# The second down projection of a decoder trunk as seven block products per group of 1024 hidden rows

## The chip, the cores and the metric

The kernel runs on one core of one Trainium2 chip. The core has five engines that run side by side, each with its own queue of instructions: PE (TensorE, matmuls), DVE (VectorE), ACT (ScalarE), POOL (GpSimd) and SP (SyncE, which here only issues DMAs). The metric is the device time of one execution in microseconds; a kernel is run several times and the median is given. Besides, one execution is profiled, and all durations of single instructions come from it.

## What is computed

The reference is a decoder trunk of two layers over 512 positions and 1024 channels. Each layer runs a token mixer (a gated DeltaNet in the first, a Conformer convolution module in the second), a cross-attention into a fixed memory and a squared-ReLU MLP; a last RMSNorm ends it. The change touches only the MLP of the second layer and the last norm behind it:

```python
def rms_norm(x, g):
    xf = x.astype(jnp.float32)
    y = xf * lax.rsqrt(jnp.mean(xf * xf, axis=-1, keepdims=True) + RMS_EPS)
    return (y * g.astype(jnp.float32)).astype(x.dtype)

def sq_relu_mlp(h, w_up, w_down):              # w_up 1024 x 4096, w_down 4096 x 1024
    return jnp.square(jax.nn.relu(h @ w_up)) @ w_down

# in reference(), for every layer
        h = h + sq_relu_mlp(rms_norm(h, mlp_norm[layer]), mlp_w_up[layer], mlp_w_down[layer])
# after the last one
    return rms_norm(h, final_norm)
```

## The kernel before

Activations lie with channels on the 128 partitions and the 512 positions ("tokens") along the free axis, so the residual is eight tiles of 128x512. Every float32 operand of a large product is split into a high part (rounded to fp32r by a copy on ACT) and a low part (the difference, on DVE); `mm3` (L236) then makes three matmuls of each product: high by high, low by high, high by low. `proj` (L246) runs `mm3` over the eight contraction tiles: 24 matmuls of 128x512 for one output tile. `split` (L275) makes the two parts of an activation tile.

Weights come as units of 128x1024 float32 (512 KB). `wload` (L197) issues the DMA of a unit from the SP queue into a tile named `raw`, of which there are `NRAW` = 3; `wsplit` (L205) makes the high part `wh` on ACT and the low part `wl` on DVE, of which there are `NW` = 3 each; `wnext` (L226) hands the next unit out and runs loads and splits ahead of it: the split of a unit stands two units ahead of its use, and needs the `wh` and `wl` tiles of the unit three before it. `plan`, `plan_mlp` (L165) and the lists around them set the order of the units. The engines' own order is made by the tile framework's scheduler, which keeps each engine first in, first out.

`mlp` (L1008) is called for both layers. The 4096 hidden channels are four groups of 1024. `MLP_ORDER` (L1562) is up 0, up 1, down 0, up 2, down 1, up 3, down 2, down 3, so that a group's down projection never follows directly on its own up projection. Each up step makes eight output tiles; `up_ev` takes one out of PSUM with a multiply by the norm's factor and a maximum with zero (DVE), squares it (ACT) and splits it (ACT, DVE). Each down step of eight output tiles adds one group's part to the residual with one DVE add per tile.

The last down step of the second layer is `finish` (L1497). There the products have the tokens on the output's partitions: the hidden tile's 128-token slices are the stationary operand and the weights, repacked in blocks of 512 output channels, are the moving one. Its order is `LAST` (L1488), eight tiles of (128 tokens) x (512 channels): four transposes with the identity bring the residual into the same PSUM bank, 24 matmuls add the product, then the final norm: a sum of squares (ACT), the root (ACT), its reciprocal and the multiply by it and by `gt` (DVE), and two DMAs to the output per token block. `load` (L1491) brings the weights of this step, outside of `wnext`.

## Time and profile before

| | us |
|---|---|
| median of 3 runs | 1502.38 |
| lowest and highest run | 1501.81, 1502.51 |
| span of the profiled execution, first to last instruction | 1500.9 |
| second MLP with the final norm, by the trace | 1142.3 to 1500.9 |

| engine | busy us | instructions |
|---|---|---|
| DVE | 894.9 | 1318 |
| ACT | 685.1 | 1202 |
| POOL | 212.2 | 223 |

The busy time of PE is made of matmuls whose ends are modelled, and matmuls overlap: one 128x512 matmul is shown as 0.39 us long, while the next starts 0.23 us after it. So PE's pace is read from the distance of starts, not from the mean duration. A group's line names the line of the source, the engine, the operation, the tiles (out<-in), the shape and the count, then busy us and the mean ns of one, and behind the second bar the engine's idle time before these instructions and what ended it. A line can be that of a helper: `tt` is L69, `stt` is L72.

### The profile page before, as it was taken

How to read it: one execution, taken by the hardware profiler on the slowest of the kernel's cores; microseconds unless marked ns; L12 is line 12 of the kernel's file. 1: busy time of each engine (PE TensorE's matmuls, PEld its weight loads, DVE VectorE, ACT ScalarE, POOL GpSimd, SP SyncE). 2: the span in 40 equal slices, each digit the busy share in tenths (PEclk: the TensorE clock that was granted, in tenths of full speed). 3: DMA queues.
4: the chain of work that ended last, by engine and by line, in shares of the span. 5: the costliest groups of instructions: out<-in, count | busy, mean ns of one | idle time of the engine just before them, and what ended most of it. 6: DMA issues, size and time to landing. Idle time of an engine off the chain costs nothing.

```text
span 1500.9 us, 19205 instructions
## 1 busy us (share of the span) xinstructions
PE 1492.3 (99%) x7458; PEld 1258.5 (84%) x7458; DVE 894.9 (60%) x1318; ACT 685.1 (46%) x1202; POOL 212.2 (14%) x223
## 2 busy tenths in 40 slices
PE   9999999999999999999999999999999999999998
PEld 7888889888888888888888889988888888888886
DVE  6889888867555543444445799976555543434441
ACT  7856765555444432322324464564444431423332
POOL 1411311102111000000002496211111000000000
PEclk9999999999999999999999999999999999999999
DMA  6231223522212332222233524532122222232321
GB/s 240 83 120 57 68 88 113 174 94 88 79 48 96 99 98 98 98 99 97 92 123 130 190 88 140 170 123 98 57 71 90 93 98 98 98 98 99 98 99 56
DMA packets 50059, 155.65 MB, mean 104 GB/s; under 512 B 6320, under 2 KB 8624, under 8 KB 49968
## 3 DMA queue, kind: packets, MB, share of 16 engines
q1 hardware_dynamic: 49536, 153.90, 30.7%
q8 instruction: 58, 0.95, 0.3%
q10 hardware_dynamic: 432, 0.52, 0.1%
q14 instruction: 33, 0.27, 0.1%
HBM read 151.52 MB, written 2.10 MB: 102 GB/s over the span
## 4 chain that ended last, share of the span: by engine, by line
PE 96%; ACT 2%; DVE 1%; issue 0%; DMA 0%; POOL 0%; SPq 0%; DVEq 0%
PE up L238 8%; PE up L240 8%; PE up L239 8%; PE dn L240 7%; PE dn L238 7%; PE dn L239 7%; PE pw L240 3%; PE pw L239 3%; PE pw L238 3%; PE h L238 3%; PE h L239 2%; PE h L240 2%; PE xo L239 2%; PE q L238 2%; PE xo L240 2%; PE q L240 2%
## 5 line engine op out<-in xcount | busy, mean ns | idle before, releaser
L214 ACT CAST wh<-raw 128x1024 fp32r<-128x1024 f32 x247 | 259.2, 1051 | 598.1 <-PE dn L239 190.4
L69 DVE TENSOR_TENSOR wl<-raw,wh 128x1024 fp32r<-128x1024 f32 (+1 forms) x238 | 290.9, 1224 | 82.9 <-ACT wh L214 76.7
L240 PE MATMUL up<-xh,wl 128*128 128x512 f32 x512 | 199.2, 389 | 0.0
L239 PE MATMUL up<-xl,wh 128*128 128x512 f32 x512 | 199.2, 389 | 0.0
L238 PE MATMUL up<-xh,wh 128*128 128x512 f32 x512 | 199.2, 389 | 0.0
L240 PE MATMUL dn<-uh,wl 128*128 128x512 f32 x448 | 174.3, 389 | 0.0
L238 PE MATMUL dn<-uh,wh 128*128 128x512 f32 x448 | 174.3, 389 | 0.0
L239 PE MATMUL dn<-ul,wh 128*128 128x512 f32 x448 | 174.3, 389 | 0.0
L69 DVE TENSOR_TENSOR h<-dn,h 128x512 f32<-128x512 f32 x56 | 41.8, 747 | 165.3 <-PE dn L240 165.3
L72 DVE SCALAR_TENSOR_TENSOR rl<-up,rb 128x512 f32<-128x512 f32 x64 | 44.2, 691 | 153.8 <-PE up L240 153.7
L69 POOL TENSOR_TENSOR sq<-sq,sq 128x512 f32<-128x512 f32 x30 | 49.3, 1644 | 485.9 <-ACT sq L331 475.6
L240 PEld LDWEIGHTS up<-xh,wl 128*128 128x128 f32 x512 | 96.1, 188 | 20.0
L239 PEld LDWEIGHTS up<-xl,wh 128*128 128x128 f32 x512 | 96.1, 188 | 20.0
L238 PEld LDWEIGHTS up<-xh,wh 128*128 128x128 f32 x512 | 96.1, 188 | 19.9
L239 PEld LDWEIGHTS dn<-ul,wh 128*128 128x128 f32 x448 | 84.1, 188 | 17.6
L240 PEld LDWEIGHTS dn<-uh,wl 128*128 128x128 f32 x448 | 84.1, 188 | 17.4
L238 PEld LDWEIGHTS dn<-uh,wh 128*128 128x128 f32 x448 | 84.1, 188 | 17.4
L1148 DVE SCALAR_TENSOR_TENSOR ca<-x,prm,ca 128x512 f32<-128x512 f32 x112 | 82.3, 752 | 3.6 <-ACT ca L1145 1.3
L238 PE MATMUL h<-xh,wh 128*128 128x512 f32 x184 | 73.7, 400 | 0.0
L240 PE MATMUL h<-xh,wl 128*128 128x512 f32 x184 | 71.9, 391 | 0.0
L239 PE MATMUL h<-xl,wh 128*128 128x512 f32 x184 | 71.7, 390 | 0.0
L72 DVE SCALAR_TENSOR_TENSOR cva<-cv,prm,cva 128x512 f32<-128x512 f32 x60 | 48.3, 830 | 11.5 <-POOL cva L69 10.3
(364 smaller groups left out, 3037.4 us busy)
## 6 DMA issues: line engine op xcount, KB each, us to landing
raw<-w_up SPq DMA_DIRECT2D x64, 512.0 KB, 3.5
raw<-w_dn SPq DMA_DIRECT2D x64, 512.0 KB, 3.4
raw<-w_pw SPq DMA_DIRECT2D x24, 512.0 KB, 3.5
raw<-w_k SPq DMA_DIRECT2D x16, 512.0 KB, 3.6
raw<-w_vv SPq DMA_DIRECT2D x16, 512.0 KB, 3.6
raw<-w_q SPq DMA_DIRECT2D x16, 512.0 KB, 3.3
raw<-w_o SPq DMA_DIRECT2D x16, 512.0 KB, 3.6
raw<-w_kq SPq DMA_DIRECT2D x15, 512.0 KB, 3.6
```

What stands on the lines that cost most here:

```text
L69: return e.tensor_tensor(out=o, in0=a, in1=b, op=op)
L72: return dve.scalar_tensor_tensor(out=o, in0=a, scalar=s, in1=b, op0=op0, op1=op1)
L214: ins = [act.copy(h, raw)]
L238: pe.matmul(ps, wh, xh, start=first, stop=False)
L239: pe.matmul(ps, wh, xl, start=False, stop=False)
L240: pe.matmul(ps, wl, xh, start=False, stop=last)
L1148: first["tap"] = dve.scalar_tensor_tensor(out=a, in0=src, scalar=w, in1=a, op0=ALU.mult, op1=ALU.add)
```

## The change

The second layer's MLP gets a function of its own, `mlp7`, in place of `mlp` with `finish`. The order becomes up 0, down 0, up 1, down 1, up 2, down 2, up 3, down 3. All four down steps now have the tokens on the output's partitions.

In a down step the 512 tokens are halved (blocks 1 and 2 of the left factor's rows), the 1024 hidden rows of the group are halved (the inner dimension; `w_up` is packed in another order so that hidden tiles alternate between the halves), and the 1024 output channels are halved. With left blocks a11, a12, a21, a22 and weight blocks b11 to b22 the four output blocks come from seven products in the form of Strassen and Winograd:

- S1 = a21 + a22, S2 = S1 - a11, S3 = a11 - a21, S4 = a12 - S2 (POOL, four operations of 128x256 for each pair of hidden tiles, in `operands`)
- T1 = b12 - b11 (DVE), T3 = b22 - b12, T2 = T3 + b11, T4 as b21 - T2 (POOL; each 128x1024, and each in two halves, in `combos7`)
- products in the order of `ORDER7`: a11 b11, S1 T1, S2 T2, S4 b22, S3 T3, a12 b21, a22 T4 (with the sign turned). Each has 24 matmuls of 128x512: two weight units of twelve. They accumulate in three pairs of PSUM banks (keys "a", "c", "b"), and `after` reads partial sums out between products and joins them with the running output `acc` (ACT copies, POOL and DVE adds).

Each of the seven right factors is split into high and low parts in two units, so a group's down step splits 14 units where it split 8. The residual is transposed tile by tile in `turn`, behind the up tiles of group 0 (eight times four transposes, as many as `finish` had). The final norm stands in `final`, which works on the SBUF tile that `done` has made with one more DVE add. The raw tiles become `RAWB` = 6 for the whole kernel; each is asked for as late in the plan as before, but a DMA can start up to three tiles earlier. T2's second half and `gt` take a raw tile too.

```diff
-    raw0 = wp.tile([P, 1024], F32, tag="raw", name="raw0", bufs=NRAW)
+    raw0 = wp.tile([P, 1024], F32, tag="raw", name="raw0", bufs=RAWB)
...
+    def plan_mlp7(layer):
+        for g in range(4):
+            for i in range(4):
+                plan(("up", layer, g * 4 + i), w_up[layer, g * 4 + i])
+            n = base7[g] = len(loads)
+            for b, h in LOADS7:
+                loads.append(w_dn[layer, g * 4 + "11 21 12 22".split().index(b)][:, h * 1024:(h + 1) * 1024])
+            at = {bh: n + i for i, bh in enumerate(LOADS7)}
+            for u in range(14):
+                order.append((("dn7", g), u))
+                need.append(max([at[bh] for bh in NEEDS7[ORDER7[u // 2][1]](u % 2)] + need[-1:]))
...
     def wsplit():
...
-        raw = ws["raw"].pop(u)
+        (kind, i, *j), hf = order[u]
+        raw = combos7(i, hf) if kind == "dn7" else ws["raw"].pop(need[u])
...
-        while ws["load"] < min(i + NRAW + 2, len(order)):
+        while ws["load"] <= need[min(i + NRAW + 1, len(order) - 1)]:
             wload()
...
+    def combos7(g, u):
+        raw, (name, h) = ws["raw"], (ORDER7[u // 2][1], u % 2)
...
+        if name == "11":
+            T7["3", h] = fs("t3")
+            tt(pool, T7["3", h], b("22"), b("12"), ALU.subtract)
+            T7["2", h] = fs("t2") if h == 0 else raw_tile("t2")
+            tt(pool, T7["2", h], T7["3", h], b("11"), ALU.add)
+            return b("11")
+        if name == "T1":
+            t = raw.pop(base + LOADS7.index(("12", h)))
+            tt(dve, t, t, raw.pop(base + LOADS7.index(("11", h))), ALU.subtract)
+            return t
...
+        if name == "21":
+            t = b("21")
+            tt(pool, T7["2", h], t, T7["2", h], ALU.subtract)
+            return raw.pop(base + LOADS7.index(("21", h)))
...
+    def mlp7(layer, norm, hres):
...
+        def turn(i):
+            n, m, c = i // 4, i // 2 % 2, i % 2
+            ps, a = psum("hT"), slot(s="acc")
             for j in range(4):
+                pe.transpose(ps[:, j * P:(j + 1) * P], hres[4 * m + j][:, n * 256 + c * P:n * 256 + c * P + P], ident)
+            act.copy(a, ps)
+            acc[n, m, c] = a
...
+        def operands(u0, u1):
+            o = {}
+            a11, a21, a12, a22 = u0[:, 0:256], u0[:, 256:512], u1[:, 0:256], u1[:, 256:512]
+            x, y = slot(s="s12"), slot(s="s34")
+            tt(pool, x[:, 0:256], a21, a22, ALU.add)
+            tt(pool, x[:, 256:512], x[:, 0:256], a11, ALU.subtract)
+            tt(pool, y[:, 256:512], a12, x[:, 256:512], ALU.subtract)
+            tt(pool, y[:, 0:256], a11, a21, ALU.subtract)
+            o["12"], o["22"] = pair(split(u1, "a"))
+            o["S1"], o["S2"] = pair(split(x, "s"))
+            o["S3"], o["S4"] = pair(split(y, "s"))
+            return o
+
+        def plain(u0):
+            t = slot(F32R, "a11")
+            act.copy(t[:, 0:256], u0[:, 0:256])
+            tt(dve, t[:, 256:512], u0[:, 0:256], t[:, 0:256].bitcast(F32), ALU.subtract)
+            return [t[:, 0:256], t[:, 256:512]]
+
+        def dn7(g, ops):
...
+                for h in range(2):
+                    w = wnext(("dn7", g), 2 * i + h)
+                    for c in range(2):
+                        ps = bank[key][c]
+                        for kk in range(2):
+                            k, s = 2 * h + kk, slice(kk * 512, kk * 512 + 512)
+                            xh, xl = [t[:, c * P:(c + 1) * P] for t in ops[k][left]]
+                            pe.matmul(ps, xh, w[0][:, s], start=opens and k == 0, stop=False, skip_group_check=True)
+                            pe.matmul(ps, xl, w[0][:, s], start=False, stop=False, skip_group_check=True)
+                            pe.matmul(ps, xh, w[1][:, s], start=False, stop=k == 3, skip_group_check=True)
+                        if h == 1:
+                            after(i + 1, c, ps)
...
+            def done(n, m, c, ps, other):
+                acc[n, m, c] = added(dve, ps, other, "acc")
+                if g == 3:
+                    final(n, m, c)
+
+            def after(i, c, ps):
+                if i == 1:
+                    t1 = slot(s="t1")
+                    act.copy(t1, ps)
+                    st["12", c] = added(pool, t1, acc[0, 1, c], "v12")
+                    st["t1", c] = t1
+                elif i == 2:
+                    t5 = slot(s="t5")
+                    act.copy(t5, ps)
+                    t = added(pool, t5, acc[1, 1, c], "v22")
+                    st["22", c] = added(pool, t, st["t1", c], "w22")
+                elif i == 3:
+                    st["12", c] = added(dve, ps, st["12", c], "u2")
+                    st["21", c] = added(pool, st["t1", c], acc[1, 0, c], "v21")
+                elif i == 4:
+                    done(0, 1, c, ps, st["12", c])
+                elif i == 5:
+                    done(1, 1, c, ps, st["22", c])
+                elif i == 6:
+                    done(0, 0, c, ps, acc[0, 0, c])
+                else:
+                    done(1, 0, c, ps, st["21", c])
...
+        def final(n, m, c):
+            x = acc[n, m, c]
...
+            act.activation(slot(s="fq"), x, AF.Square, accum_out=ss)
...
+            act.activation(sd, ss, AF.Sqrt, bias=b, scale=1.0 / 1024)
             dve.reciprocal(rc, sd)
+            act.activation(y1, y1, AF.Copy, scale=rc)
+            stt(y, x, rc, gt[0][:, gs], ALU.mult, ALU.mult)
...
+        for g in range(4):
+            ops, us = [{} for _ in range(4)], []
+            for i in range(8):
+                w = wnext(("up", layer, g * 4 + i // 2), i % 2)
+                ps = psum("up")
+                proj(w, xs, ps, inside={1: norm.stat} if (g, i) == (0, 1) else None)
...
+                if g == 0 and i > 1:
+                    turn(i - 2)
+            if g == 0:
+                turn(6)
+                turn(7)
...
+            dn7(g, ops)
...
+RAWB = 6
+LOADS7 = [(_b, _h) for _h in range(2) for _b in ("11", "12", "22")] + [("21", 0), ("21", 1)]
+ORDER7 = [("11", "11", "a", True), ("S1", "T1", "c", True), ("S2", "T2", "b", True), ("S4", "22", "c", False),
+          ("S3", "T3", "b", False), ("12", "21", "a", False), ("22", "T4", "b", False)]
...
-    nc = _bacc.Bacc("TRN2", target_bir_lowering=False, num_devices=1)
+    nc = _bacc.Bacc("TRN2", target_bir_lowering=False, num_devices=1, dynamic_dma_scratch_size=1024)
```

More of the change, by code (lines that the diff above doesn't have):

```diff
@@ L142, in tile_trunk, with put @@
     pool.memset(eps_ln, LN_EPS)
-    order, srcs = [], {}
+    order, srcs, loads, need = [], {}, [], []
+    def put(key, hf, src=None):
+        order.append((key, hf))
+        loads.append((srcs[key] if src is None else src)[:, hf * 1024:(hf + 1) * 1024])
+        need.append(len(loads) - 1)
     def plan(key, src, n=2):
@@ L192, in tile_trunk, with raw_tile @@
     plan_x(1)
-    plan_mlp(1, True)
+    plan_mlp7(1)
     ws = {"next": 0, "split": 0, "load": 1, "raw": {0: raw0}, "hl": {}}
+    def raw_tile(s="raw"):
+        return wp.tile([P, 1024], F32, tag="raw", name=nm(s), bufs=RAWB)
     def wload():
         u = ws["load"]
-        key, hf = order[u]
         ws["load"] += 1
-        raw = wp.tile([P, 1024], F32, tag="raw", name=nm("raw"), bufs=NRAW)
-        nc.sync.dma_start(out=raw, in_=srcs[key][:, hf * 1024:(hf + 1) * 1024])
+        raw = raw_tile()
+        nc.sync.dma_start(out=raw, in_=loads[u])
         ws["raw"][u] = raw
@@ L1005, in xattn, with mlp @@
         return new
-    def mlp(layer, norm, hres, nxt, mid=None, end=None, pre=None):
+    def mlp(layer, norm, hres, nxt, mid):
         xs = norm.xs
@@ L1021, in mlp @@
         for kind, g in MLP_ORDER:
-            if (kind, g) == ("dn", 3) and mid is not None:
+            if (kind, g) == ("dn", 3):
                 mid()
-            if (kind, g) == ("dn", 3) and end is not None:
-                return end(hid[3], cur)
             for i in range(8):
@@ L1533 @@
+    mlp7(1, n5, h)
 NSLOT = 69
@@ L1649, in _layout @@
     r["w_o"] = np.stack([_pack_a(np, i["xa_w_o"][j]) for j in range(2)])
[L1650 to L1651 removed]
+    halves = [8 * g + m for g in range(4) for m in (0, 4, 1, 5, 2, 6, 3, 7)]
+    r["w_up"] = np.stack([_pack_a(np, i["mlp_w_up"][j], halves if j else None) for j in range(2)])
+    r["w_dn"] = np.stack([np.concatenate([(_pack_b if j else _pack_a)(
         np, i["mlp_w_down"][j][g * 1024:(g + 1) * 1024]) for g in range(4)]) for j in range(2)])
```

117 lines of the change are left out of this document (68 added, 49 removed).

## The prediction

> **What bounds the kernel now.** I read the page first: the busy lines, the clock and the chain that ended last.
>
> ```profile
> PE 1492.3 (99%) x7458; PEld 1258.5 (84%) x7458; DVE 894.9 (60%) x1318; ACT 685.1 (46%) x1202; POOL 212.2 (14%) x223
> PEclk9999999999999999999999999999999999999999
> PE 96%; ACT 2%; DVE 1%; issue 0%; DMA 0%; POOL 0%; SPq 0%; DVEq 0%
> ```
>
> PE makes 96% of the chain at full clock, DMA and the SP queue 0%. Whether it is also dense in the second MLP, the timeline and the groups of 1131 to 1456 us say.
>
> ```profile
> 1142.33 0.39 PE L238 MATMUL up<-xh,wh 128*128 128x512 f32 x1
> ...
> 1152.35 0.39 PE L238 MATMUL up<-xh,wh 128*128 128x512 f32 x1
> ...
> 1157.79 0.39 PE L238 MATMUL up<-xh,wh 128*128 128x512 f32 x1
> ...
> 1459.67 0.48 PE L1510 MATMUL dn<-wdh,uh 128*128 128x512 f32 x1
> ...
> 1465.02 0.39 PE L1512 MATMUL dn<-wdl,uh 128*128 128x512 f32 x1
> ...
> 1465.60 0.47 PE L1510 MATMUL dn<-wdh,uh 128*128 128x512 f32 x1
> ...
> 1494.61 0.39 PE L1512 MATMUL dn<-wdl,uh 128*128 128x512 f32 x1
> ```
>
> The second and third row are 24 matmuls apart: 5.44 us, 0.2267 us each. The next three frame one tile of `finish`: 24 matmuls and four transposes in 5.93 us, so the transposes cost 0.49. The MLP's 64 tiles of 24 matmuls make 348.2 us, the norm's two matmuls 0.5, eight times 0.49 is 3.9: 352.6. From the first row to the end of the last one's slot, 1494.84, are 352.5: there is not one hole. The token-first form runs at the same pace as the other. What a matmul less saves here is 0.2267 us, as long as everything else keeps up.
>
> ```profile
> L69 DVE TENSOR_TENSOR wl<-raw,wh 128x1024 fp32r<-128x1024 f32 x56 | 68.6, 1225 | 14.8 <-ACT wh L214 14.7
> L214 ACT CAST wh<-raw 128x1024 fp32r<-128x1024 f32 x56 | 59.0, 1053 | 194.8 <-PE up L239 94.7 <-PE dn L239 87.5 <-issue 12.6
> L69 DVE TENSOR_TENSOR ul<-u,uh 128x512 fp32r<-128x512 f32 x32 | 22.1, 692 | 2.8 <-ACT uh L277 2.7
> L277 ACT CAST uh<-u 128x512 fp32r<-128x512 f32 x32 | 19.9, 622 | 1.0
> L72 DVE SCALAR_TENSOR_TENSOR rl<-up,rb 128x512 f32<-128x512 f32 x32 | 22.1, 691 | 76.9 <-PE up L240 76.8
> L69 DVE TENSOR_TENSOR h<-dn,h 128x512 f32<-128x512 f32 x24 | 16.6, 691 | 73.8 <-PE dn L240 73.8
> ```
>
> ACT waits for PE to give `wh` back before nearly every split, and DVE's `rl` and `h` wait for PE: both have room.
>
> **What goes from PE.** Before, a down step has 8 x 24 = 192 matmuls, after it 7 x 24 = 168: 4 x 24 = 96 fewer, 96 x 0.2267 = 21.8 us. The transposes move from the end to group 0 and stay 32: 0.
>
> The Trainium skill, "TensorE: Matmul & The Clock Gate", section "Wait — 56ns, not 53.3ns?", gives a warm matmul N/2.4 GHz plus about 2.5 ns, 215.8 ns at N = 512; by it the saving is 20.7 us, an estimate. The trace's 226.7 differs and decides.
>
> **What comes on DVE, ACT and POOL.** Per group DVE has 22 `wl` (27.0), two T1 halves (2.5), eight `rl` (5.5), twelve splits of 128x512 and four of 256 (9.7) and ten adds from PSUM (6.9): 51.6 us in a group of 43.5 + 38.1 = 81.6 (15 x 5.44). ACT has 22 x 1.053 and some 16 of smaller work, 39. For POOL the trace has these rows, in the whole kernel, in the window 1131 to 1456, and in a stretch where DVE is full:
>
> ```profile
> L69 POOL TENSOR_TENSOR wl<-raw,wh 128x1024 fp32r<-128x1024 f32 x13 | 31.1, 2403 | 9.3 <-ACT wh L214 9.3
> L69 POOL TENSOR_TENSOR ca<-ca,cvp 128x512 f32<-128x512 f32 x30 | 42.7, 1423 | 30.9 <-ACT cvp L1133 23.3 <-ACT cvp L1131 6.1
> L69 POOL TENSOR_TENSOR pexp<-pexp,sm 128x512 f32<-128x512 f32 x16 | 17.7, 1108 | 123.0 <-DVE sm L937 123.0
> L69 POOL TENSOR_TENSOR sq<-sq,sq 128x512 f32<-128x512 f32 x2 | 3.5, 1766 | 7.3 <-ACT sq L331 7.3
> 884.00:908.00 24.00, 24.00 (x124) 20.34 (x123) 23.47 (x34) 13.58 (x28) 21.45 (x13) 1.00 0.25 79
> L1148 DVE SCALAR_TENSOR_TENSOR ca<-x,prm,ca 128x512 f32<-128x512 f32 x27 | 19.8, 752 | 0.5
> ```
>
> A 1024-wide operation (A): 2.40 by the same shape, up to 2 x 1.77 = 3.53. A 256-wide one (B) has no row: half of a 512-wide one, 0.55 to 0.89; I take 0.7. Per group 6 A, 16 B and eight of 512: 37 us, at most 50, of 81.6. No engine becomes the bound by its sum; what counts is who waits in a queue.
>
> **A weight unit lasts half as long.** In a down step a unit now feeds 12 matmuls, 2.72 us, not 5.44. Its split may start when the unit three before is done, two units (5.44 us) before its use, and takes 1.05 + 1.23 + about 0.2 of hand-over: 2.5. Cover 2.9 us, less what stands ahead of it. In the built order those are at most two ACT copies (t1, t5; 1.2) or two DVE adds (1.4). I cost it at 0; with the cover gone, each late microsecond shows.
>
> **The step from up to down.** Before, a whole up step lay between the last `up_ev` of a group and its first use. Now the down step follows at once. Counting from the start of an up step (group 1 on), the weight half (22, 1) takes the raw tile of up unit 7, whose split begins when unit 4 is done, 27.2; it ends at 29.7, and with 3.4 us of DMA
>
> ```profile
> raw<-w_dn SPq DMA_DIRECT2D x64, 512.0 KB, 3.4
> ```
>
> it is there at 33.2. POOL's queue is then T3, three S operations of the third pair, T2, the fourth S: 33.2 + 2A + 4B. Behind that S stands ACT's copy of it (0.62), behind this on DVE its low part (0.69), the `rl` of up tile 6 (0.69) and `wl` of down unit 1 (1.23): 3.45 with hand-overs. PE needs that `wl` for the third matmul of unit 1, at 43.5 + 2.72 + 0.45 = 46.7. So nothing is late if 2A + 4B is under 10.0. With my values it is 7.6, at the upper ends 10.6: 0.6 to 0.8 late in each group, some 3 us in all. The last pair's S1 is needed 39 matmuls (8.8 us) into the down step; `rl`, square, three B, ACT and DVE end at about 6. In group 0 three of the transposes stand before the down step and give 1.5 us more. Bounds 0 to 3; I take 0.5, since the row of the same shape says 0.
>
> **The end.** These are the last instructions before:
>
> ```profile
> 1495.03 0.60 ACT L1514 ACTIVATE fq<-dn 128x512 f32<-128x512 f32 x1 [5.22 <-PE dn L1512]
> 1495.53 0.19 ACT L1514 ACTIVATION_READ_ACCUMULATOR fq<-dn 128x1 f32 x1
> 1495.75 0.29 ACT L1523 ACTIVATE sm<-sm,sm 128x1 f32<-128x1 f32 x1
> 1496.08 0.16 DVE L1524 RECIPROCAL sm<-sm 128x1 f32<-128x1 f32 x1 [5.49 <-ACT sm L1523]
> 1496.35 0.75 DVE L72 SCALAR_TENSOR_TENSOR y<-dn,sm,gt 128x512 f32<-128x512 f32 x1
> 1497.12 0.33 SPq L1528 DMA_DIRECT2D yT<-y  x1
> ```
>
> PE ends at 1495.0, the last multiply at 1497.1: 2.1 us; the rest (DMA, end) stays. Afterwards four tiles are normed last, two of product 6 and two of product 7. DVE's built order is add, reciprocal, multiply, four times over, so the next add waits for the last tile's root on ACT. One turn: add 0.69 and hand-over 0.1, then 2.07 as above: 2.86. The first add stands behind the `wl` of the last unit (13), whose `wh` tile is free at 11 x 2.72 = 29.9 from the start of the down step; 1.05 on ACT, and on DVE it follows `wl` 12 and a `y`: it ends at about 32.5. Then 32.5 + 4 x 2.86 = 43.9, against PE's end at 38.1: 5.8, or 3.7 more than before. From below, if only the last two turns chain: the first tile ends six matmuls before PE, -1.36 + 2 x 2.86 + 0.1 = 4.5, 2.4 more. From above, DVE's add of product 5 waits for POOL: T4 half 0 waits for a DMA at 16.9 (its raw tile is that of b22, free after unit 6), and T4 twice and four adds at 3.53 and 1.77 end at 31.1; `wl` 13 then ends near 34.8: 6.0 more.
>
> **Six raw tiles.** Up to the second MLP the built order of PE, DVE, ACT and POOL is unchanged, only SP issues weights earlier. With DMA at 0% of the chain: 0, from -1 to +1.
>
> **Sum**, against the profiled execution: 1500.9 - 21.8 + 0.5 + 3.7 = 1483.3. The runs lie 1502.38 - 1500.9 = 1.5 above it: 1484.8. By its bounds (saving 21.8; tail 2.4 to 6.0; step 0 to 3; loads -1 to 1) 1482.0 to 1491.6.
>
> **Rivals.** *POOL and DVE get in each other's way at the step from up to down.* If DVE instructions with two inputs and POOL could not run at once, POOL's queue after 33.2 would also wait for DVE's `wl`, T1 and two low parts, 1.23 + 1.23 + 1.38 = 3.8: 7.6 + 3.8 = 11.4, 1.4 late, and the last pair as much again: about 2 to 3 per group, 10 in all: 1495. Against it: in the 24 us above POOL is busy 21.45, and DVE 23.47, 19.8 of that in `ca` with two inputs at 752 ns, no longer than the 0.75 us of the multiply at 1496.35, when POOL is idle. Chance 0.13, with all slower POOL rows.
>
> The rule behind it is in the Trainium skill, "SBUF — State Buffer", section "Who interferes with whom": the two share a port pair that one holds for a whole instruction, the other fully blocks. The trace does not agree: 21.45 and 23.47 do not fit in 24.00 one after the other.
>
> *The split of weights becomes the bound of the down steps.* Three `wh` tiles, so a unit takes at least a third of (2.72 + split time). At 2.5 that is 1.7, hidden under 2.72. It decides from 5.44 on, and the gain is gone when a unit takes 17.6 / 56 = 0.31 more, 3.03, at a split time of 6.4. At 7 it is 3.24: 56 x 0.52 = 29.1, so 1484.8 + 29.1 = 1514. For it: 24 more splits, and DVE adds that wait for POOL stand ahead of `wl` in one queue. Against it: 4.5 us of waiting in every unit, on an engine with 51.6 of 81.6 filled. Chance 0.10.
>
> *The gain is eaten*, a unit late by 0.3 us or every step by 4: 1502, chance 0.05.
>
> **How the numbers follow.** Forecast 0.72, with its own range 1481.5 to 1491; rivals 0.13, 0.10, 0.05. The range reaches to the first rival: 1481.5 to 1496, leaving out the two last and some of the first. What this measurement can tell from no change is about 0.2%, 3 us. Faster 0.72 + 0.13 = 0.85; of the last case 0.04 is within the 3 us, 0.01 beyond, so same 0.04 and slower 0.11.
>
> **What would show it.** Right: up and down matmuls 0.227 us apart over all of the MLP, about 1142 to 1473; idle DVE and ACT still waiting for PE; four turns of add, reciprocal and multiply of 2.9 us at the end, PE ending 5.8 us before the last multiply and some 9.6 before the end of the span. Wrong: holes on PE behind ACT's or DVE's splits at unit 1 of a down step (the step), or every 2.72 us (the splits); POOL's 1024-wide operations over 3.5 us; DVE's `wl` well over 1.23; a change before 1142.

## The result, and the profile after

| | before | after |
|---|---|---|
| median of 4 runs, us | 1502.29 | 1509.57 |
| lowest to highest, us | 1501.81 to 1502.51 | 1509.19 to 1509.70 |
| span of the profiled execution, us | 1500.9 | 1508.0 |

The changed kernel takes 1.0050 times as long, with a 95% interval of 1.0036 to 1.0064: slower by half a per cent, where 1484.8 us and faster were forecast. Its page has these three lines, the busy times, the granted clock and the chain that ended last:

```profile
PE 1480.8 (98%) x7362; PEld 1243.9 (82%) x7362; DVE 1019.0 (68%) x1390; ACT 736.2 (49%) x1274; POOL 413.8 (27%) x343
...
PEclk9999999999999999999999999999999999999999
...
PE 83%; DVE 5%; POOL 4%; ACT 3%; issue 3%; DMA 1%; DVEq 0%; POOLq 0%
```

PE had 96% of the chain before. The 96 matmuls are gone (7458 to 7362), but 17% of the chain now lies outside PE, with DVE and POOL ahead of all others. The page's clock digits hide what happens: a slice of 38 us rounds a stretch of 3 us away.

Two rows of the timeline, the first and the last matmul of the MLP, give its length, 354.54 us in place of 352.28 before:

```profile
1141.67 0.39 PE L291 MATMUL up<-xh,wh 128*128 128x512 f32 x1
...
1496.21 0.39 PE L1595 MATMUL dn<-wl,ah 128*128 128x512 f32 x1
```

Without a hole it would be 352.28 - 21.77 = 330.51, so 24.0 us are lost inside the MLP. Behind the last matmul's start lie 1508.0 - 1496.21 = 11.8 us, before 1500.9 - 1494.61 = 6.3: 5.5 more. And the MLP starts 0.7 earlier. -21.8 + 24.0 + 5.5 - 0.7 = +7.0, against +7.1 between the spans.

The groups by line and shape between 1142 and 1508 us, with busy time and mean ns of one behind the first bar, show what became slow:

```profile
L69 DVE TENSOR_TENSOR wl<-raw,wh 128x1024 fp32r<-128x1024 f32 x62 | 99.7, 1619 | 9.6 <-ACT wh L234 9.4
...
L69 DVE TENSOR_TENSOR wl<-t,wh 128x1024 fp32r<-128x1024 f32 x24 | 43.2, 1820 | 5.2 <-ACT wh L234 5.2
...
L69 DVE TENSOR_TENSOR sl<-s,sh 128x512 fp32r<-128x512 f32 x32 | 33.2, 1041 | 28.9 <-ACT sh L330 27.4
...
L69 POOL TENSOR_TENSOR t<-raw,t 128x1024 f32<-128x1024 f32 x8 | 27.3, 3418 | 0.0
...
L69 POOL TENSOR_TENSOR s<-u 128x256 f32<-128x256 f32 x16 | 20.6, 1290 | 0.0
...
L69 POOL TENSOR_TENSOR t<-raw,raw 128x1024 f32<-128x1024 f32 x8 | 20.6, 2572 | 29.5 <-DMA raw<-w_dn 28.0 <-DVE sl L69 1.5
```

`wl` took 1225 ns before, now 1619 and 1820 on average; a low part of 512 columns goes from 692 to 1041. POOL's 1024-wide operations are 2572 to 3418 (taken at 2400), its 256-wide ones up to 1290 (taken at 700). DVE and POOL are slow together.

How that reaches PE is to be followed in group 2, whose up step starts at 1321.99. First the middle of that step, on DVE, POOL and ACT:

```profile
1339.36 2.69 POOL L69 TENSOR_TENSOR t<-raw,raw 128x1024 f32<-128x1024 f32 x1 [0.95 <-DVE sl L69]
...
1340.31 2.82 DVE L69 TENSOR_TENSOR wl<-raw,wh 128x1024 fp32r<-128x1024 f32 x1
...
1342.13 3.26 POOL L69 TENSOR_TENSOR t<-t,raw 128x1024 f32<-128x1024 f32 x1
...
1343.06 2.62 DVE L69 TENSOR_TENSOR a<-u,a 128x256 fp32r<-128x256 f32 x1
...
1347.44 0.63 ACT L1554 ACTIVATE u<-rl 128x512 f32<-128x512 f32 x1 [2.66 <-DVE rl L72]
```

The four operations pass in turn: T3 ends at 1342.05, `wl`, which began inside it, at 1343.13, T2, which began inside that, at 1345.39, and DVE's difference of 256 columns, which takes 0.42 elsewhere, at 1345.68. DVE has lost 1.6 and 2.2 us, `rl` of the next tile is late, and ACT has waited 2.66 us for it. The S of that pair, ACT's copies of it and the `wh` behind them all move back (the four S operations run from 1348.16 to 1351.80 and the copies from 1351.01), and the split of up unit 7, whose tile the half (22, 1) takes over, ends 32.9 us after the start of the step, not 29.7. The rest of the chain follows in the timeline, from the DMA that SP issues when that split is done:

```profile
1354.94 18.81 SPq L221 DMA_DIRECT2D raw<-w_dn  x3
...
1358.70 2.39 POOL L69 TENSOR_TENSOR t<-raw,raw 128x1024 f32<-128x1024 f32 x1 [6.90 <-DMA raw<-w_dn]
...
1361.04 0.74 POOL L69 TENSOR_TENSOR s<-u,u 128x256 f32<-128x256 f32 x1
...
1361.74 1.72 POOL L69 TENSOR_TENSOR s<-u 128x256 f32<-128x256 f32 x1
...
1363.42 1.18 POOL L69 TENSOR_TENSOR s<-s,u 128x256 f32<-128x256 f32 x1
...
1364.57 2.40 POOL L69 TENSOR_TENSOR t<-t,raw 128x1024 f32<-128x1024 f32 x1
...
1366.93 1.19 POOL L69 TENSOR_TENSOR s<-u,s 128x256 f32<-128x256 f32 x1
...
1368.15 0.62 ACT L330 CAST sh<-s 128x512 fp32r<-128x512 f32 x1 [2.89 <-POOL s L69]
...
1368.67 1.04 ACT L234 CAST wh<-raw 128x1024 fp32r<-128x1024 f32 x1
```

The DMA lands at 1358.70, 36.7 after the start and not 33.2; the four S operations take 4.83 and not 2.8. ACT waits for the fourth, and the weights of unit 1 stand behind it. PE, in the same stretch:

```profile
1368.01 0.39 PE L1595 MATMUL dn<-wl,a 128*128 128x512 f32 x1
1369.77 0.50 PE L1593 MATMUL dn<-wh,a 128*128 128x512 f32 x1 [1.37 <-ACT wh L234]
...
1371.28 0.50 PE L1595 MATMUL dn<-wl,a 128*128 128x512 f32 x1 [0.78 <-DVE wl L69]
...
1372.41 0.63 PE L1595 MATMUL dn<-wl,a 128*128 128x512 f32 x1
1372.84 0.63 PE L1593 MATMUL dn<-wh,a 128*128 128x512 f32 x1
```

Two holes of 1.53 and 0.94 us, and after them starts 0.43 apart, not 0.227. The view by windows, whose column before the last two is the granted clock, says why:

```profile
1371.60:1375.00 3.40, 3.40 (x10) 2.63 (x9) 3.19 (x5) 2.74 (x4) 2.01 (x2) 0.51 0.57 176
1375.20:1379.00 3.80, 3.80 (x18) 3.13 (x18) 2.38 (x3) 1.96 (x3) 2.35 (x2) 1.00 0.68 227
```

For 3.4 us the clock was 0.51: ten matmuls lie in them, wholly or in part, and eighteen in the 3.8 us after. At half pace 3.4 us hold 1.7 us of work, so the two holes, 2.5 us, cost up to another 1.7. The changed kernel has four such stretches in the MLP, one in each group.

Group 0 lost more than group 2. The four down steps take 46.41, 42.74, 42.40 and 44.77 us from their first matmul to the next up step (the last one to its last matmul's start). The kernel with everything on DVE, shown further down, needs 38.19, 38.08, 38.08 and 37.85. So 8.2, 4.7, 4.3 and 6.9 us were lost, 24.1 in all. In group 0, whose down step starts at 1189.32, PE stands at units 0, 1 and 3; the two longest waits:

```profile
1195.86 0.50 PE L1595 MATMUL dn<-wl,a 128*128 128x512 f32 x1 [1.83 <-DVE wl L69]
...
1203.36 0.50 PE L1593 MATMUL dn<-wh,sh 128*128 128x512 f32 x1 [2.15 <-ACT wh L234]
```

The `wl` that the first row waits for stands on DVE behind two low parts that take 3.80 us beside T2. The `wh` of the second row stands on ACT behind the copies of the last pair's S, which POOL makes from 1197.81 to 1201.71. Besides, `turn`'s copies of the transposes stand in ACT's queue behind a copy of S, and PE waits 0.98 us for one of them at unit 0.

### The profile page after: what moved, and what is told of

Read it like the earlier page. It is cut to its first block, busy times and chain, and to the rows that moved or that the text cites. A ratio compares the mean times of both kernels' runs of the same rounds, so it can differ in the third digit from the quotient of the medians.

```text
span 1508.0 us, 19404 instructions
## 1 busy us (share of the span) xinstructions
PE 1480.8 (98%) x7362; PEld 1243.9 (82%) x7362; DVE 1019.0 (68%) x1390; ACT 736.2 (49%) x1274; POOL 413.8 (27%) x343
## 4 chain that ended last, share of the span: by engine, by line
PE 83%; DVE 5%; POOL 4%; ACT 3%; issue 3%; DMA 1%; DVEq 0%; POOLq 0%
PE up L291 5%; PE up L292 5%; PE up L293 5%; PE dn L293 4%; PE dn L291 4%; PE dn L292 4%; PE pw L291 3%; PE pw L293 3%; PE pw L292 3%; POOL s L69 3%; PE dn L1595 3%; PE dn L1594 3%; PE dn L1593 3%; PE h L291 3%; PE h L292 2%
## 5 line engine op out<-in xcount | busy, mean ns | idle before, releaser
L234 ACT CAST wh<-raw 128x1024 fp32r<-128x1024 f32 x255 | 267.6, 1051 | 473.5 <-PE up L292 124.5
L69 DVE TENSOR_TENSOR wl<-raw,wh 128x1024 fp32r<-128x1024 f32 (+1 forms) x246 | 324.5, 1323 | 77.7 <-ACT wh L234 71.2
L291 PE MATMUL dn<-uh,wh 128*128 128x512 f32 x256 | 99.6, 389 | 0.0
L292 PE MATMUL dn<-ul,wh 128*128 128x512 f32 x256 | 99.6, 389 | 0.0
L293 PE MATMUL dn<-uh,wl 128*128 128x512 f32 x256 | 99.6, 389 | 0.0
L69 DVE TENSOR_TENSOR h<-dn,h 128x512 f32<-128x512 f32 x32 | 25.2, 788 | 91.5 <-PE dn L293 91.5
L292 PEld LDWEIGHTS dn<-ul,wh 128*128 128x128 f32 x256 | 48.1, 188 | 10.1
L293 PEld LDWEIGHTS dn<-uh,wl 128*128 128x128 f32 x256 | 48.1, 188 | 9.9
L291 PEld LDWEIGHTS dn<-uh,wh 128*128 128x128 f32 x256 | 48.1, 188 | 9.9
```

The source lines that it names most:

```text
L69: return e.tensor_tensor(out=o, in0=a, in1=b, op=op)
L234: ins = [act.copy(h, raw)]
L291: pe.matmul(ps, wh, xh, start=first, stop=False)
L292: pe.matmul(ps, wh, xl, start=False, stop=False)
L293: pe.matmul(ps, wl, xh, start=False, stop=last)
```

## The experiments

Below, "S" stands for all S operations, "T" for T2, T3 and T4, and "the adds" for POOL's eight of 512 columns per group. "MLP" in the table is the distance from the first up matmul to the last down matmul in each profile, as above; the ratio is to the kernel before in the same set of runs.

| kernel | MLP us | median us | ratio, 95% interval |
|---|---|---|---|
| before | 352.28 | 1502.29 | |
| after | 354.54 | 1509.57 | 1.0050 (1.0036 to 1.0064) |
| S on DVE | 334.34 | 1489.02 | 0.9906 (0.9890 to 0.9923) |
| T on DVE | 352.63 | 1506.82 | 1.0028 (1.0017 to 1.0039) |
| S and T on DVE | 332.05 | 1487.11 | 0.9897 (0.9882 to 0.9911) |
| after, other order at the end | 353.50 | 1506.60 | 1.0028 (1.0017 to 1.0038) |
| S and T on DVE, other order at the end | 331.86 | 1484.94 | 0.9880 (0.9864 to 0.9897) |
| T half 1 behind S in POOL's queue | 350.50 | 1506.87 | 1.0028 (1.0017 to 1.0040) |
| everything on DVE, other order at the end | 330.41 | 1482.62 | 0.9876 (0.9861 to 0.9891) |
| the same, S alone back on POOL | 345.92 | 1499.29 | 0.9979 (0.9969 to 0.9988) |
| the same, T alone back on POOL | 346.15 | 1498.71 | 0.9979 (0.9970 to 0.9989) |
| before with six raw tiles | 352.28 | 1502.61 | 1.0003 (0.9994 to 1.0011) |

**Work taken from POOL.** The first three move S, then T, then both:

```diff
-            tt(pool, x[:, 0:256], a21, a22, ALU.add)
+            tt(dve, x[:, 0:256], a21, a22, ALU.add)
...
-            tt(pool, T7["3", h], b("22"), b("12"), ALU.subtract)
+            tt(dve, T7["3", h], b("22"), b("12"), ALU.subtract)
```

> The changed kernel with the four S operations of each pair (sums and differences of hidden tiles) on DVE, not POOL; T2, T3, T4 and the eight 512-wide adds stay on POOL. Theory A (the loss in the MLP is the first weight units of each down step: S of the last pairs stands behind T3, which waits for a DMA, in POOL's queue; ACT's copy of S and DVE's low part stand behind that in theirs, and each hole of over 1.5 us on PE is followed by some 3.4 us of matmuls at half pace): with the S operations out of POOL's queue, at least two thirds of the 24.0 us lost in the MLP go; holes of PE at units 1 and 2 of a down step under 0.5 us in sum per group; 0.427 us pace gone; the end unchanged (PE's end to span end 11.5): 1509.6 - 16 to 20 = 1489 to 1494. Rival B (DVE, busy 1019 of 1508, or the split of weights is the limit of the down steps, and the POOL rows are only a symptom): DVE gets 16 x 4 operations of 256 columns more, some 24 us; slower than the changed kernel: 1512 to 1520.

> The changed kernel with T2, T3 and T4 (1024-wide combinations of weight blocks, six per group) on DVE, not POOL; the S operations stay on POOL. Theory A: S of the last pairs no longer waits behind T3's DMA on POOL; but T3 half 1 now waits for the DMA of (22,1) in DVE's queue, with the low parts of the third pair behind it, so the step is better but perhaps not clear of holes: 1490 to 1500. Rival B (DVE or the split of weights is the limit): 6 x 1.2 = 7 us more on DVE per group, 29 in all: 1515 to 1525. If POOL and DVE taking turns over two-input operations is what stretches DVE's wl from 1.22 to 1.62, it falls to about 1.35 here and in the first kernel of this set to about 1.5.

> The changed kernel with both the S operations and T2, T3, T4 on DVE; POOL keeps eight 512-wide adds per group. Theory A with its second part (DVE and POOL take turns, so POOL's work costs DVE nearly as much time as doing it itself): DVE's wl back at 1.25 to 1.3, its busy time up by less than the 53 us of moved work at DVE's pace, holes at the step gone: 1487 to 1493, the best of the three or level with the first. Rival B (DVE is the limit): the slowest of the three, 1520 or more. Rival C (no exclusion, only POOL's queue order): level with the first kernel of the set, wl still at 1.6.

With both on DVE the time was 1487.1, the best of the three, as the theory with its second part said. With S on DVE alone 20.2 of the 24.0 us come back, as the first theory said, and rival B (DVE is full) falls: DVE got more work and the kernel 20 us faster. But two things went against the theory. With T on DVE no S stands behind a DMA any more, and still only 1.9 us come back: 1506.82 lies outside both expectations. And `wl` came down less than expected: with S and T on DVE to 1404 and 1594 ns (for units read from `raw` and from `t`), not to 1.25 or 1.3 us, and with S alone on DVE not at all. In these two groups of that kernel it is as slow as in the changed kernel, or slower:

```profile
L69 DVE TENSOR_TENSOR wl<-raw,wh 128x1024 fp32r<-128x1024 f32 x62 | 98.9, 1605 | 7.0 <-ACT wh L234 6.7
...
L69 DVE TENSOR_TENSOR wl<-t,wh 128x1024 fp32r<-128x1024 f32 x24 | 50.2, 2113 | 1.6 <-ACT wh L234 1.6
```

**Do DVE and POOL take turns?** The kernel before was given made-up work on POOL: three operations with two inputs beside each tile of the first MLP, six fills beside each tile of the second.

```diff
...
+                tt(pool, dum[0][:, 0:1], dum[1][:, 0:1], w[0][:, 0:1].bitcast(F32), ALU.mult)
+                for _ in range(3 if layer == 0 else 6):
+                    if layer == 0:
+                        tt(pool, dum[0], dum[0], dum[1], ALU.mult)
+                    else:
+                        pool.memset(dum[0], 0.0)
...
```

> The kernel before with made-up work on POOL (its result is used by nothing): beside each of the 64 tiles of the first MLP three POOL additions-like operations with two inputs of 128x512, beside each of the 64 of the second MLP six POOL fills of 128x512, which read nothing; DVE's and ACT's work is unchanged, and the scratch size is that of the changed kernel. Taking turns over two-input operations: in the first MLP DVE's wl goes from 1.22 to 1.6 or more, ul and h up as well where both inputs lie in SBUF, rl and h (one input from PSUM) stay at 0.69, POOL's operation goes from 1.28 alone to about 2; in the second MLP wl stays at 1.22 to 1.25. Rival (any POOL traffic slows DVE): wl is stretched in both. Rival (no influence, as I read the trace of before): wl 1.22 in both, POOL 1.1 to 1.4. PE is not the loser in any case, as before: 1502 +- 2; and if the scratch size alone cost time, 1505 or more.

The groups by line and shape, first of the first MLP (475 to 735 us), then of the second (1152 to 1456):

```profile
L69 POOL TENSOR_TENSOR dum<-dum,dum 128x512 f32<-128x512 f32 x140 | 216.3, 1545 | 11.0
...
L69 DVE TENSOR_TENSOR wl<-raw,wh 128x1024 fp32r<-128x1024 f32 x48 | 74.4, 1551 | 9.5 <-ACT wh L217 9.3
...
L69 DVE TENSOR_TENSOR ul<-u,uh 128x512 fp32r<-128x512 f32 x31 | 42.2, 1360 | 2.7 <-ACT uh L280 2.7
...
L72 DVE SCALAR_TENSOR_TENSOR rl<-up,rb 128x512 f32<-128x512 f32 x31 | 21.4, 690 | 44.0 <-PE up L243 43.9
```

```profile
L1037 POOL MEMSET dum<- 128x512 f32 x323 | 169.9, 526 | 18.6
...
L69 DVE TENSOR_TENSOR wl<-raw,wh 128x1024 fp32r<-128x1024 f32 x53 | 64.9, 1225 | 16.5 <-ACT wh L217 16.5
```

Beside two-input work on POOL, `wl` goes from 1225 to 1551 and `ul` from 692 to 1360. POOL's own operation is at 1545, not the 2 us expected. `rl`, one of whose inputs lies in PSUM, stays at 690. Beside fills, which read nothing, `wl` is 1225 to the nanosecond. So what collides here is a DVE instruction with both inputs in SBUF and a POOL instruction that reads SBUF. That holds for the other DVE operation with two tensors too; one pair of this run's timeline, in which the multiply takes 1.77 where the same form takes 0.75 with POOL idle:

```profile
469.74 2.27 POOL L69 TENSOR_TENSOR sq<-sq,sq 128x512 f32<-128x512 f32 x1
...
470.79 1.77 DVE L72 SCALAR_TENSOR_TENSOR xl<-h,prm,xh 128x512 fp32r<-128x512 f32 x1
```

The Trainium skill, "SBUF — State Buffer", section "Who interferes with whom", says that a DVE instruction with two SBUF inputs contends with a GpSimd instruction that reads SBUF and not with one that only writes it. It also says that a DVE instruction with at most one SBUF input, outside the 2-port perf modes, does not contend. The rows here agree: 1551 and 1360 ns beside `dum<-dum,dum`, 1225 beside the fills, 690 for `rl`.

The time, 1509.3 for one run, missed the expected 1502. The second MLP starts at 1148.97, 6.6 later than before, and itself takes 352.27 us as before. Most of the 6.6 is lost in the token mixer: the made-up work keeps POOL busy until 828.12, the squares of the mixer's norm come behind it, and PE waits 3.08 us for their copy at 833.98, with a half clock of 3.41 us behind.

**The order of POOL's queue.** Here all work stays where the change put it, only the second half's T2 and T3 are issued behind the last pair's S:

```diff
...
+        if name == "11" and h == 1:
+            return b("11")
+        if name == "T1" and h == 1:
+            t = raw.pop(base + LOADS7.index(("11", 1)))
+            tt(dve, t, b("12"), t, ALU.subtract)
+            T7["2", 1], T7["3", 1] = raw_tile("t2"), fs("t3")
+            with tc.issue_after(ws["s"].ins):
+                tt(pool, T7["2", 1], b("22"), t, ALU.subtract)
+                tt(pool, T7["3", 1], b("22"), raw.pop(base + LOADS7.index(("12", 1))), ALU.subtract)
+            return t
...
```

> All work stays on POOL and DVE as in the changed kernel, only POOL's queue is re-ordered for the second half of the weights: T2 (now computed as b22 - T1, T1 formed in the tile of b11) and T3 are issued behind the S operations of the last pair, so no S waits behind the DMA of (22,1). Theory A (the order of the queue is the cause): the holes at unit 1 of groups 1 to 3 (2.5 to 2.8 us each, with some 2 us of half pace behind) are gone; 1509.6 - 12 to 16 = 1494 to 1498; POOL's operations and DVE's wl are as slow as before (wl 1.6, T 2.4 to 3.4). Rival D (taking turns is the cause, the DMA wait is not): T2 and T3 still hold DVE and the holes stay or move to units 2 to 5: 1504 to 1512.

The holes at unit 1 of groups 1 to 3 went, as both expected. A new one of 1.95 us came at unit 4 of each, with a stretch at half clock behind it, and 4.0 of the 24.0 us are all that came back in the profiled execution (the medians differ by 2.7): rival D. In the timeline of group 1:

```profile
1289.17 3.51 DVE L69 TENSOR_TENSOR sl<-s,sh 128x512 fp32r<-128x512 f32 x2 [1.28 <-ACT sh L340]
...
1289.26 5.67 POOL L69 TENSOR_TENSOR t<-raw,raw 128x1024 f32<-128x1024 f32 x2
...
1292.60 5.63 DVE L69 TENSOR_TENSOR wl<-t,wh 128x1024 fp32r<-128x1024 f32 x2
```

Two low parts that take 1.4 together take 3.51 beside T2 and T3, and two `wl` 5.63 in place of 2.45. So the wait for the DMA was not the cause by itself: with it out of S's way, the turns stop PE three units later.

**The end.** The reciprocal and the multiply of a tile are issued behind the next tile's add:

```diff
                 acc[n, m, c] = added(dve, ps, other, "acc")
+                was = late[:]
+                late.clear()
                 if g == 3:
                     final(n, m, c)
+                for f in was:
+                    f()
...
```

> The changed kernel with only the order at the end changed: the reciprocal and the multiply of a normed tile are put behind the add of the next tile, so DVE's adds no longer wait for the root of the tile before. My term for the end (four chained turns of add, reciprocal, multiply): PE's last matmul to the last multiply falls from 7.1 us to about 3.5 (last add 0.7, square and root 1.3, reciprocal, multiply 1.0, hand-overs), time 1509.6 - 3.5 = 1506. Rival (the end is set by the weight splits ahead of the first add, or by the last DMA): under 1 us of gain. Holes of PE in the middle stay as they are.

> S, T2, T3 and T4 on DVE (1487.1 measured) together with the new order at the end: the two gains add up, 1487.1 - 3.4 = 1483.7, the span behind the last matmul 10.7 - 3.4 = 7.3 us. Rival (with DVE fuller the end has no room): 1486 to 1487.

The time went from 1509.57 to 1506.60 alone, 3.0 us, and from 1487.11 to 1484.94 with S and T on DVE, 2.2 us. In the profiles the part behind the last matmul's start became 2.55 us shorter alone (11.75 to 9.20) and 2.45 with S and T on DVE (11.06 to 8.61). So the turns were a real term, of the same size in both kernels; the difference between 3.0 and 2.2 is within the intervals of the table. From PE's end to the last multiply it is 3.35 us in place of 7.13, as expected. The second kernel came out above the expected 1483.7, with 8.2 us behind PE's end and not 7.3.

**Is the half clock a matter of the holes alone?** The kernel before was given waits for PE, made of ACT copies; the dummy matmul that waits adds nothing to the result.

```diff
...
+            for j in range(n1):
+                act.activation(dum[0], dum[0] if j else ps, AF.Copy, scale=0.0)
...
+                if n1:
+                    pe.matmul(ps, dum[0][:, 0:P], dum[0], start=True, stop=True)
...
```

> The kernel before, with waits made for PE out of ACT copies: seven single ones in the second MLP (1, 2, 3, 4, 5, 7 and 10 copies of about 0.6 us, each some 40 us after the last) and seven pairs in the first MLP, two waits a few matmuls apart. POOL and DVE work as before. Theory: the half pace of the matmuls (0.427 us apart in place of 0.227, for 2 to 4 us) follows from the holes of PE alone: it comes after single holes above some length between 2 and 3 us and after pairs with more than about 2.2 us in sum, not after the shorter ones; each such stretch costs 1.3 to 1.9 us on top of the hole. Holes sum up to some 35 to 40 us; with the half pace 1545 to 1560. Rival (the half pace came from POOL's or DVE's traffic or from late weights, not from holes): no matmul 0.427 us apart here, 1535 to 1542.

In this run POOL is idle in the second MLP and DVE as fast as before. After a hole of 1.6 us the clock stayed at 1.00, after one of 2.2 it fell in one case of three, after each of 2.9 or more it fell. Two of the dummies, each with its wait, and the windows behind them:

```profile
1192.18 0.50 PE L1039 MATMUL up<-dum 128*128 128x512 f32 x1 [1.41 <-ACT dum L1025]
...
1286.60 0.79 PE L1039 MATMUL dn<-dum 128*128 128x512 f32 x1 [2.73 <-ACT dum L1025]
```

```profile
1192.00:1196.00 4.00, 3.82 (x17) 3.16 (x18) 2.18 (x3) 1.38 (x3) 0.00 (x0) 1.00 0.39 131
1287.00:1293.00 6.00, 6.00 (x15) 4.60 (x15) 0.00 (x0) 0.00 (x0) 0.00 (x0) 0.52 0.25 85
```

So the holes bring it, whoever makes them. But the length of a hole alone does not decide. In the kernel with T alone back on POOL, three holes of 2.4 us end at 1294.84, 1381.34 and 1466.83; the clock falls behind the first and stays at 1.00 behind the other two. And the hole of 1.99 us in group 0 of the changed kernel, at 1195.86, brings no fall. The pairs of waits gave nothing to read, since other matmuls were moved into the second one. The sum of the holes was larger than I had planned, so the time of the one run, 1573 us, missed the expected 1545 to 1560 and tells nothing more.

**Everything on DVE, and one part back.** `v` and `w` of `after` go to DVE too, so that POOL is idle in the second MLP; then S alone, and T alone, go back.

```diff
...
-                    st["12", c] = added(pool, t1, acc[0, 1, c], "v12")
+                    st["12", c] = added(dve, t1, acc[0, 1, c], "v12")
...
```

> The kernel with S, T2, T3, T4 on DVE and the new order at the end (1484.9 measured), and now POOL's last work too, the eight 512-wide adds per group, on DVE: POOL is idle in the second MLP. If DVE and POOL take turns over two-input operations, POOL's adds cost DVE about what doing them itself costs: wl falls from 1.40 (raw) and 1.59 (t) to 1.22 to 1.23, which gives back 62 x 0.18 + 24 x 0.37 = 20 us, against 32 x 0.69 = 22 us of adds: DVE's busy time 1026 +- 5 as before, time 1483 to 1486. Rival (POOL's adds were nearly free for DVE): DVE busy +22 us, and holes at units 2 to 5 from the adds in its queue: 1488 or more.

> The kernel with everything on DVE and the new end (1482.6 measured), with only the S operations back on POOL. After the runs so far (T off POOL alone gave back 2 of the 24.0 us lost in the MLP, T behind S 4, S off POOL 20) the theory is: what costs is that S goes over POOL at all, since ACT's copy of S and DVE's low part stand in ACT's and DVE's queues ahead of the next weight splits, and S takes some 4.7 us there in place of 1.7. Then this run loses at least 6 us: 1489 to 1500, with holes at the first units of the down steps. Rival (S is harmed only by the company of T or of the adds on POOL): 1482 to 1486, no holes.

> The same kernel with only T2, T3 and T4 back on POOL. Theory as in the run beside it: no activation waits for them and no weight split but their own, so although they stretch wl they cost 0 to 4 us: 1482 to 1487. Rival (taking turns with T's long operations is what breaks the step, whoever makes S): 1492 or more.

The page and two groups of the kernel with everything on DVE:

```profile
PE 1470.6 (99%) x7362; PEld 1240.2 (84%) x7362; DVE 1020.2 (69%) x1510; ACT 735.1 (50%) x1274; POOL 212.2 (14%) x223
```

```profile
L69 DVE TENSOR_TENSOR wl<-raw,wh 128x1024 fp32r<-128x1024 f32 x62 | 75.8, 1222 | 11.9 <-ACT wh L234 11.5
...
L69 DVE TENSOR_TENSOR wl<-t,wh 128x1024 fp32r<-128x1024 f32 x24 | 29.1, 1221 | 6.4 <-ACT wh L234 6.0
```

POOL has 212.2 us, as in the kernel before, where the changed kernel had 413.8. DVE has taken over all of that work, 201.6 us as POOL did it and some 78 at DVE's pace (64 S operations at 0.42 us, 24 of T at 1.22, 32 adds at 0.69), and is busy for 1020.2 us, against 1019.0. So in sum POOL's work had cost DVE as much as doing it itself. `wl` is back at 1222. And the MLP takes 330.41 us, 21.87 less than before.

With S back 15.5 us are lost in the MLP, with T back 15.7. For S the time was expected; the place was not, since the holes are at units 3, 5 and 6 and not at the first ones. `wl` is hardly stretched in that kernel (1241 and 1220 ns). What is late is S itself: the last pair's four operations take 4.6 us on POOL, where DVE makes them in 1.7, and PE waits for ACT's copy of S. In group 1, whose down step starts at 1275.94:

```profile
1285.94 0.50 PE L1593 MATMUL dn<-wh,sh 128*128 128x512 f32 x1 [0.31 <-ACT sh L330]
```

For T the expectation missed and its rival, 1492 or more, came out. The timeline of that kernel shows why: here no S stands on POOL, but the adds stand on DVE.

```profile
1371.55 2.79 POOL L69 TENSOR_TENSOR t<-raw,t 128x1024 f32<-128x1024 f32 x1 [13.96 <-DVE wl L69]
...
1371.99 2.89 DVE L69 TENSOR_TENSOR v<-t,acc 128x512 f32<-128x512 f32 x1
```

An add of 0.68 us takes 2.89, since T4 began 0.44 earlier; the next `wl` stands behind it, and PE has its holes at units 5 and 6, which follow. So neither S's place nor T's is the cause by itself. POOL's work costs time in two ways here: its operations stretch those of DVE, T's above all, and S, which PE waits for, comes later. How much of S's delay is POOL's own pace and how much the turns was not separated: one S operation takes at least 0.73 us on POOL, 1.0 to 1.3 on average in the kernel with S alone there, and 0.42 on DVE.

The kernel with S alone on DVE, which keeps T and the adds on POOL, loses only 3.8. Its timeline fits the same account. In group 2 the last pair's low part ends at 1365.97 and the third weight split behind it at 1373.80, 7.8 us later. With the adds on DVE and T alone on POOL the two ends are 1372.07 and 1383.75, 11.7 us apart, with six adds among the splits.

**Six raw tiles.** The kernel before with `bufs=6` in place of `NRAW`, and the smaller DMA scratch of the changed kernel:

```diff
...
-        raw = wp.tile([P, 1024], F32, tag="raw", name=nm("raw"), bufs=NRAW)
+        raw = wp.tile([P, 1024], F32, tag="raw", name=nm("raw"), bufs=6)
...
```

> The kernel before with six raw tiles in place of three and the smaller scratch, nothing else. My term was 0, from -1 to +1: 1501.5 to 1503.5. Rival (the change's profile reached the second MLP 0.66 us sooner because of the raw tiles): 1501.0 to 1501.9, and its second MLP starts before 1142.0 in the profile.

No difference (1.0003, 0.9994 to 1.0011). Its profile does start the second MLP at 1141.55; but the kernels above, with the same code up to there, start it anywhere from 1141.46 to 1145.89, so the 0.7 us of the changed kernel's profile mean nothing.

## Why the prediction was wrong, step by step

- **What goes from PE: right.** 21.8 us were predicted, and 21.87 is what the MLP lost where nothing is late.
- **A weight unit lasts half as long, costed at 0:** small. In group 3 of the changed kernel holes of 0.56, 1.07 and 0.60 us lie at its last units, 2.2 in all; with S and T on DVE there is none in that group, so they too hang on POOL's work.
- **The step from up to down, 0.5 with bounds 0 to 3: this step failed.** With its half clock it takes some 22 of the 24 us lost: 8.2 in group 0, 4.7 and 4.3 in groups 1 and 2, and 4.7 of the 6.9 in group 3. The form of the sum was right, and its wide ends not far off: 2A + 4B came to 2.39 + 2.40 + 4.83 = 9.6 in group 2, under the 10.0 that I had allowed. What broke it there is the origin. I had the DMA of (22, 1) at 33.2; in the trace it lands at 36.7, because S and the first half's T3 and T2 on POOL had already put ACT and DVE back. With POOL idle the count is right: in the kernel with everything on DVE, group 2's up step starts at 1308.90 and the DMA lands 33.18 after it.

```profile
1342.08 1.23 DVE L69 TENSOR_TENSOR t<-raw,raw 128x1024 f32<-128x1024 f32 x1 [3.36 <-DMA raw<-w_dn]
```

  With S alone back on POOL it lands at 35.0 in that group, with T alone at 34.5, so each brings about half of the delay. Then 36.7 + 9.6 + 3.2 of copies behind it is 49.5, against 46.7: 2.8 late, which is the two holes, 2.5. Two more parts of the step were mis-sized. The last pair's S1, costed at about 6 us into the down step against a need at 8.8, is ready at 12.7 in group 2, just before PE, late by then, asks for it at 13.2; with POOL idle it is 8.3. And group 0, which I had given 1.5 us more room, lost most: its copies of the transposes stand on ACT behind those of S.
- **The first rival was right in its mechanism, and I dismissed it on a misread row.** It was priced at 1495 with a chance of 0.13. Against it stood the `ca` row, 752 ns on DVE in a stretch where POOL was busy for 21.45 of 24 us. But that `ca` is an accumulator in PSUM (line 1144 of the kernel before takes it from `psum`), so it has one input in SBUF. Its name does not say so, and POOL's `ca` of the same name is another tile. So 21.45 and 23.47 did not have to fit into 24.00 one after the other, and the trace of before did not speak against the rule. By the Trainium skill, "SBUF — State Buffer", section "Who interferes with whom", a DVE instruction with at most one SBUF input does not contend with GpSimd outside the 2-port perf modes, and `rl` at 690 ns agrees; I had read the rule as "any two inputs". The same 24 us of the trace of before held a row that spoke for the rule: `glu`, a multiply of the same form as `ca` but with both tensors in SBUF, took 1.00, where 0.75 is its time with POOL idle.
```profile
894.94 1.00 DVE L72 SCALAR_TENSOR_TENSOR glu<-pa,prm,sg 128x512 f32<-128x512 f32 x1
```

- **Priced too low even so.** The rival counted 2 to 3 us a group, at the end of the step only. It left out the same turns earlier in the queue (the origin above), and the granted clock, which halves after the holes and for which I had no term at all: up to 1.7 us behind the 2.5 us of group 2, and some 6 in the four stretches of the MLP.
- **The end, 3.7: undersized, 5.5 measured.** The mechanism, four chained turns, is there, with 2.66 for one in place of 2.86: the adds start at 1492.98, 1495.64, 1498.31 and 1500.97.

```profile
1492.98 0.68 DVE L69 TENSOR_TENSOR acc<-dn,acc 128x512 f32<-128x512 f32 x1
```

  PE ends at 1496.6, so the first add starts 3.6 us before PE's end and not 5.6. It stands behind the last unit's `wl`, and that unit's `wh` stands on ACT behind a square of the norm, which waits for DVE's add before it; I had let ACT start as soon as the tile was free. The order of the turns explains 2.5 of the 5.5, by the runs with the other order.
- **Six raw tiles, 0: right.**
- **The splits as the bound, 1514, and the gain eaten, 1502:** the time came out between the two, for another reason. In no group does the trace show a hole in every unit.
- **The bounds of the sum:** the upper ones add up to 1502.38 - 21.8 + 6.0 + 3 + 1 = 1490.6, not 1491.6. Nothing hangs on it.

## What to carry to other kernels

Before work is put on POOL beside a full DVE, look at where each operand lies: if both of DVE's inputs and POOL's are in SBUF, the two took turns here, and the work was better done on DVE, which took over what had kept POOL busy for 201.6 us with its own busy time unchanged. A row that is to show that two engines don't disturb each other must have the operands of the case in question, which the name of a tile does not tell. And when a step depends on a chain through several first-in-first-out queues, its origin deserves the same bounds as its terms.

## What the runs showed that was not expected

- Even POOL's adds, which nothing but DVE's later adds waits for, cost DVE as much as making them: when the 32 adds, 22 us at DVE's pace, came over to DVE, its busy time went from 1023.8 to 1020.2 us (S and T on DVE with the other order, then everything).
- PE's clock falls to about half after holes shorter than I would have thought: after single ones of 2.9 us or more always, after 2.4 in one case of three, after 2.2 in one of three, after 1.95 in all three cases of the kernel with T behind S, not after 1.99 in group 0 of the changed kernel, never after 1.6 alone, and after a pair of 1.53 and 0.94 with two matmuls between. The half clock lasts 3.41 us each time in the changed kernel, and 3.41, 6.83 or 10.24 in the kernel with made holes, a part of which can lie in the hole itself. In the changed kernel's MLP the stretches begin 81.9, 85.3 and 85.3 us apart, which are 24, 25 and 25 times 3.41; so it may matter where a hole falls on such a grid, which no run here tests. The Trainium skill, "TensorE: Matmul & The Clock Gate", section "Wait — 56ns, not 53.3ns?", gives a cold start-to-start of 426.7 ns at N = 512; the 0.43 here agrees.
- A kernel faster than both came out of it: everything on DVE with the other order at the end, 1482.62 us, 0.9876 of the time before (0.9861 to 0.9891). That is near the 1484.8 forecast for the change itself: the MLP is shorter by 21.87 us and the part behind its last matmul's start 2.0 longer (8.31 in place of 6.31).
